# mLSTM running maxima and decays: broadcast by DMA and masked on GpSimd instead of selected and masked by TensorE products

## The chip, the core and the metric

One core of a Trainium2 chip runs the whole program. The metric is the device time of one execution in microseconds (us), the median of several runs.

The engines are named as in the profile: PE is TensorE (matmuls; PEld its weight loads), DVE is VectorE, ACT is ScalarE, POOL is GpSimd, SP is the engine whose queue issues most DMAs. TensorE writes to PSUM, ScalarE and VectorE read it.

## The reference, cut to what matters

The program is one inference step of a two-layer backbone for 128 prompt tokens and 256 latent tokens (three tiles of 128), width 1024. A layer normalises and modulates the tokens, mixes them with three groups of heads that share one input projection (neighbourhood attention, grouped-query attention, a bidirectional mLSTM of 4 heads of size 64), projects back, and applies a SwiGLU. The part around the change is the mLSTM, for each direction and head:

```
b    = cumsum(log_f)
logw = where(causal, b[t] - b[s] + i[s], -inf)
m_t  = max(max_s logw, b + m)                  # running maximum
s    = (q k^T) * exp(logw - m_t)
num  = s v + exp(b + m - m_t) * (C q)          # the decay of the carried state
den  = sum(s) + exp(b + m - m_t) * (n q)
h    = num / max(|den|, exp(-m_t))
```

With a[s] = i[s] - b[s] and M[t] the running maximum of a (started from m), the exponent is a[s] - M[t] where the mask allows it, and the decay is exp(m - M[t]).

## The kernel before, in words

All 384 tokens are on hand at once, and weights stream from HBM. Each projection weight is loaded as fp32 (`raw`, SP's queue), split into a high and a low part (`hi` by ScalarE, line 121; `lo` by VectorE, line 122), and multiplied in three products (`mm3`, lines 111 to 113).

The work of a mixer layer is a hand-written order of steps in `SCHEDULE`, one string a layer; within it TensorE, VectorE and ScalarE execute in the order in which the steps issue. GpSimd's and SP's queues are ordered by a planner. Steps that matter here: `f`, a part of the projections; `t`, a part of the modulation vectors (its sum is in a PSUM tile of tag `sm`); `s`, a part of the norms of heads; `rexp`, `cols`, `krow`, `rsplit`, `cin`, `decay`, `kw`, `cout`, `ogate`, parts of the mLSTM that run once a layer; `E0` to `E3`, `C0` to `C3`, `U0` to `U3`, the exponents, scores and sums of the four mLSTM units. A unit is a pair of heads (j) in one direction (dr).

The rows `m.R1` (the running maxima M, 64 x 384), `m.R2` (a) and `m.R3` hold a head's tokens along the free dimension, at partition 32 dr + head. `cols` transposes R2 and R3 so that a[s] can be a per-partition bias. To have M[t] along the free dimension of all 128 partitions, the kernel multiplies on TensorE:

- `rsplit` splits R1 into a high and a low part, `m.Rh`.
- `m_expo` (step E) multiplies a column of the negated identity `nidr`, broadcast to 128 columns, by Rh: -M[t] in all partitions, into the PSUM tile `E` (tag `pt`). Two more products per head add the mask `trir` through the identity. ScalarE then writes W = exp(E + a[s]), six instructions (line 864).
- `decays` does the same for m - M[t] into `dps` (tag `pt`) for the 64 partitions of each head; ScalarE's exponent gives `decq`, which VectorE multiplies by q.

`m_score` (step C) multiplies keys by queries into the PSUM tile `S` (tag `sc`), and VectorE multiplies W by S (line 877). `m_sum` (step U) sums over keys on TensorE into `nd` (tag `sm`), together with decq times the carried state `CT` that `cin` made out of `Craw`. The PSUM tags `sc`, `pt` and `sm` have one buffer each, `w` (the projections' sums) three. SBUF tiles of tag `m4` (Rm, Rw, Craw, decq, kw, W, ...) share three buffers.

`Ada.gate` already broadcasts a row by way of DRAM: GpSimd stores it to `row` (line 209) and loads it to all 128 partitions as `G` (line 210).

Of the kernel before, what the change touches and what calls it, by code (L numbers as in the profile page):

```python
# [16 lines left out]
D = 1024  # L17
# [29 lines left out]
C_ID, C_SC, C_MNEG, C_COS, C_SIN, C_NID, C_SI, C_SF, C_FL, C_END = (  # L47
    0, 128, 132, 196, 324, 452, 516, 580, 644, 772)
# [3 lines left out]
def hybrid_step(  # L52
# [54 lines left out]
    identr = cp.tile([128, 128], F32R, name="identr")  # L107
    nidr = cp.tile([64, 64], F32R, name="nidr")
    trir = cp.tile([128, 2, 128], F32R, name="trir")
# [154 lines left out]
    def ada_start(pp):  # L264
        """First layer's shift and scale, two feature tiles at a time."""
# [56 lines left out]
    def half_sum(n, h, ss):  # L322
        """Towards 1 / root mean square of two halves of a row, in ss[:, 0]."""
# [48 lines left out]
    def mixers(l, ma, mp, mn, pp, banks, h1T, steps, pairs, tails):  # L372
# [40 lines left out]
        def ahead(n):  # L413
            """Keeps n pairs of weights split before their use, and the loads after them under way."""
# [53 lines left out]
        def tok_first(c0):  # L468
            ps = [pp.tile([128, 512], F32, tag="w", name="tps") for _ in range(3)]
            if l == 0:  # L470
# [27 lines left out]
                xt = [norm_x(0), norm_x(1), norm_x(2, ma.tile([128, D], F32, tag="m4", name="xn2", bufs=3))]  # L498
# [23 lines left out]
                tri = tp.tile([128, 256], F32, tag="g2", name="tri", bufs=4)  # L522
                SP.dma_start(tri, consts[:, C_END:C_END + 256])
                late.enter_context(tc.issue_after(an))
                late.enter_context(tc.issue_after(v))
                V.tensor_copy(identr, ident)
                V.tensor_copy(nidr, cst[0:64, C_NID:C_NID + 64])
                V.tensor_copy(trir, tri.rearrange("p (a b) -> p a b", a=2))
# [18 lines left out]
        # ---- M: mLSTM projections  # L547
# [39 lines left out]
        grows = ma.tile([128, 384], F32, tag="m4", name="grows", bufs=3)  # L587
# [11 lines left out]
        # ---- G: rotary tables with the gains  # L599
# [127 lines left out]
        def out_first():  # L727
            ps, w = {}, {}
            for half, ch, i in [(0, 0, i) for i in range(3)] + [
# [6 lines left out]
                if ch:  # L736
                    if not half:
                        oP.append(ma.tile([128, D], F32, tag="m4", name="oP", bufs=3))
# [18 lines left out]
        # ---- M: gates  # L757
        def gates():
# [3 lines left out]
            m.R1 = mp.tile([64, 384], F32, name="R1")  # L762
# [51 lines left out]
        # ---- M: columns, final states of the prompt  # L814
# [26 lines left out]
        def m_blocks(dr):  # L841
            if dr == 0:
                return [(0, 0, 128, 0), (1, 128, 384, 128), (2, 256, 384, 384)]
            return [(0, 0, 128, 0), (1, 128, 256, 128), (2, 128, 384, 256)]

        def m_expo(u):
            j, dr = pairs_of[u]
            E = pp.tile([128, 2, 512], F32, tag="pt", name="E")
            bl = [(0, 384, 0), (256, 384, 384)] if dr == 0 else [(0, 256, 0), (128, 384, 256)]
            for hd in range(2):  # L850
                r = 32 * dr + 2 * j + hd
                sel = nidr[:, r:r + 1].broadcast_to([64, 128])
                for n, (ta, tb, o) in enumerate(bl):
                    for a in range(2):
                        PE.matmul(E[:, hd, o:o + tb - ta], lhsT=sel, rhs=m.Rh[:, a, ta:tb],
                                  start=n == 0 and a == 0, stop=False)
                PE.matmul(E[:, hd, 0:256].rearrange("p (b t) -> p b t", b=2), lhsT=identr,
                          rhs=trir[:, dr].unsqueeze(1).broadcast_to([128, 2, 128]), start=False, stop=False)
                PE.matmul(E[:, hd, 384:512], lhsT=identr, rhs=trir[:, dr], start=False, stop=True)
            M["W", u] = W = ma.tile([128, 2, 512], F32, tag="m4", name="W", bufs=3)  # L860
            for hd in range(2):
                r = 32 * dr + 2 * j + hd
                for st, ta, tb, o in m_blocks(dr):
                    A.activation(W[:, hd, o:o + tb - ta], E[:, hd, o:o + tb - ta], AF.Exp, bias=m.cols[:, st, r:r + 1])

        def m_score(u):
            j, dr = pairs_of[u]
            S = pp.tile([128, 2, 512], F32, tag="sc", name="S")
            for st, ta, tb, o in m_blocks(dr):
                for ch in range(2):  # L870
                    for hd in range(2):
                        pr = slice(64 * hd, 64 * hd + 64)
                        cc = 64 * ((ch + hd) % 2)
                        PE.matmul(S[cc:cc + 64, hd, o:o + tb - ta], lhsT=kTm[pr, j, st * 128 + cc:st * 128 + cc + 64],
                                  rhs=qTm[pr, j, ta:tb], start=True, stop=True)
# [3 lines left out]
        def m_sum(u):  # L879
# [4 lines left out]
            plan = ([(0, [(0, 0)]), (1, [(1, 128)]), (2, [(1, 256), (2, 384)])] if dr == 0  # L884
                    else [(0, [(0, 0)]), (1, [(1, 128), (2, 256)]), (2, [(2, 384)])])
# [18 lines left out]
            else:  # L904
                ht = ma.tile([128, 3, 2, 64], F32, tag="m4", name="ht", bufs=3)
# [16 lines left out]
        def decays():  # L922
            nid = cst[0:64, C_NID:C_NID + 64]
            dps = pp.tile([128, 2, 512], F32, tag="pt", name="dps")
            for dr in range(2):
                for j in range(2):
                    for hd in range(2):
                        r = 32 * dr + 2 * j + hd
# [562 lines left out]
```

## Time and profile before

| | |
|---|---|
| median of 3 runs | 1025.33 us (1025.22 to 1027.11) |
| span of the profiled execution | 1023.0 us |
| time around that span, to the median of the runs | 2.3 us |
| TensorE busy | 995.2 us, 97% |
| VectorE busy | 620.6 us, 61% |
| ScalarE busy | 469.4 us, 46% |
| GpSimd busy | 60.4 us, 6% |
| moved by DMA | 162.26 MB, mean 159 GB/s |

The span runs from the first to the last instruction of one profiled execution. Busy is the time in which an engine executed something; matmuls are pipelined and overlap, so that TensorE's work is better read from the starts of successive instructions. An idle engine that is not the bottleneck costs nothing; a wait is attributed to the work that ended last before it.

### The profile page before, as it was taken

To read this page: it belongs to the slowest core of one execution; us is meant where nothing else is said; L and a number is where in the kernel's file an instruction comes from. 1 tells how busy PE (TensorE), PEld (TensorE's weight loads), DVE (VectorE), ACT (ScalarE), POOL (GpSimd) and SP (SyncE) were. 2 spreads that over 40 slices of the span, in tenths; PEclk is the share of its full clock that TensorE was granted. 3 is DMA by queue.
4 is the path that set the end of the run, shared out by engine and by line. 5 is a ranking of instruction groups with operands and counts; after the bars stand their busy time and mean duration, and the time that the engine had idled before them with its cause. 6 is when DMAs were issued, how large, how long until landed. Compare 5 with 4: busy or idle time off the path is not lost.

```text
span 1023.0 us, 16943 instructions
## 1 busy us (share of the span) xinstructions
PE 995.2 (97%) x6777; PEld 861.1 (84%) x6777; DVE 620.6 (61%) x1035; ACT 469.4 (46%) x936; POOL 60.4 (6%) x110
## 2 busy tenths in 40 slices
PE   5999999999999999999999999999999999999997
PEld 4778887667999998989987789866799999999996
DVE  3566546667883898976255755666878533333324
ACT  4444424668733333333266444577873323333322
POOL 0310112000000300000010221000000000000000
PEclk9999999999999999999999999999999999999999
DMA  9955568425773777765033662441477344333001
GB/s 324 302 161 168 145 174 270 134 62 189 261 251 124 253 253 225 251 217 162 1 98 101 199 207 48 108 109 42 136 258 244 125 145 144 124 124 124 22 1 62
DMA packets 126831, 162.26 MB, mean 159 GB/s; under 512 B 15184, under 2 KB 89536, under 8 KB 126752
## 3 DMA queue, kind: packets, MB, share of 16 engines
q1 hardware_dynamic: 122256, 154.22, 48.1%
q0 software_dynamic: 4128, 6.80, 2.2%
q8 instruction: 53, 0.87, 0.3%
q10 hardware_dynamic: 368, 0.16, 0.1%
q14 instruction: 26, 0.21, 0.1%
HBM read 158.50 MB, written 2.66 MB: 158 GB/s over the span
## 4 chain that ended last, share of the span: by engine, by line
PE 87%; ACT 4%; DVE 4%; DMA 3%; issue 2%; DVEq 0%; SPq 0%; ACTq 0%
PE gups L111 11%; PE gups L113 11%; PE gups L112 11%; PE facc L111 6%; PE facc L113 6%; PE facc L112 6%; PE tps L111 3%; PE fps L111 2%; PE tps L113 2%; PE tps L112 2%; PE fps L113 2%; PE fps L112 2%; DMA sraw<-in_w_ada_dram 2%; PE sc L997 2%; PE ops L111 2%; PE ptp L1028 2%
## 5 line engine op out<-in xcount | busy, mean ns | idle before, releaser
L122 DVE TENSOR_TENSOR lo<-raw,hi 128x1024 fp32r<-128x1024 f32 x98 | 119.3, 1223 | 66.7 <-ACT hi L121 66.4
L121 ACT ACTIVATE hi<-raw 128x1024 fp32r<-128x1024 f32 x98 | 103.2, 1058 | 90.9 <-PE facc L113 87.1
L111 PE MATMUL gups<-hT,ring 128*128 128x384 f32 x416 | 141.1, 339 | 0.0
L113 PE MATMUL gups<-hT,ring 128*128 128x384 f32 x416 | 140.6, 338 | 0.0
L112 PE MATMUL gups<-hT,ring 128*128 128x384 f32 x416 | 140.4, 338 | 0.0
L182 DVE SCALAR_TENSOR_TENSOR spare<-araw,scol,spare 128x512 f32<-128x512 f32 x168 | 115.8, 748 | 3.7 <-DMA araw<-in_w_ada_dram 3.7
L111 PE MATMUL facc<-hi,f 128*128 128x512 f32 x240 | 95.9, 399 | 0.0
L113 PE MATMUL facc<-hi,f 128*128 128x512 f32 x240 | 94.7, 394 | 0.0
L112 PE MATMUL facc<-lo,f 128*128 128x512 f32 x240 | 94.6, 394 | 0.0
L111 PEld LDWEIGHTS gups<-hT,ring 128*128 128x128 f32 x416 | 78.1, 188 | 0.9 <-issue 0.2
L112 PEld LDWEIGHTS gups<-hT,ring 128*128 128x128 f32 x416 | 78.2, 188 | 0.3
L113 PEld LDWEIGHTS gups<-hT,ring 128*128 128x128 f32 x416 | 78.1, 188 | 0.0
L111 PE MATMUL gups<-hT,xring 128*128 128x384 f32 x224 | 76.0, 339 | 0.0
L113 PE MATMUL gups<-hT,xring 128*128 128x384 f32 x224 | 75.7, 338 | 0.0
L112 PE MATMUL gups<-hT,xring 128*128 128x384 f32 x224 | 75.6, 338 | 0.0
L111 PE MATMUL tps<-hi,hT 128*128 128x512 f32 (+1 forms) x192 | 68.5, 357 | 2.2 <-DVE hT L489 2.2
L113 PE MATMUL tps<-hi,hT 128*128 128x512 f32 (+1 forms) x192 | 65.1, 339 | 0.0
L112 PE MATMUL tps<-lo,hT 128*128 128x512 f32 (+1 forms) x192 | 65.1, 339 | 0.0
L1217 ACT ACTIVATE ring<-spare 128x1024 fp32r<-128x1024 f32 x26 | 27.6, 1060 | 60.8 <-PE gups L112 38.2
L1217 ACT ACTIVATE ring<-rgu 128x1024 fp32r<-128x1024 f32 x26 | 27.6, 1060 | 59.5 <-PE gups L112 34.6
L111 PEld LDWEIGHTS facc<-hi,f 128*128 128x128 f32 x240 | 45.1, 188 | 11.2 <-issue 1.8
L1232 DVE TENSOR_TENSOR sg<-sg,gups 128x384 f32<-128x384 f32 x40 | 22.2, 554 | 52.9 <-PE gups L113 52.9
(318 smaller groups left out, 2057.1 us busy)
## 6 DMA issues: line engine op xcount, KB each, us to landing
araw<-in_w_ada_dram SPq DMA_DIRECT2D x80, 512.0 KB, 4.5
raw<-in_w_down_dram SPq DMA_DIRECT2D x44, 512.0 KB, 4.6
raw<-in_w_in_dram SPq DMA_DIRECT2D x40, 512.0 KB, 5.0
rgu<-in_w_gu_dram SPq DMA_DIRECT2D x20, 1024.0 KB, 5.5
spare<-in_w_gu_dram SPq DMA_DIRECT2D x20, 1024.0 KB, 6.9
sraw<-in_w_ada_dram SPq DMA_DIRECT2D x16, 512.0 KB, 9.3
raw<-in_w_out_dram SPq DMA_DIRECT2D x8, 512.0 KB, 5.3
G<-row POOLq DMA_DIRECT2D x8, 512.0 KB, 5.7
```

Source lines behind the costliest of these rows:

```text
L111: PE.matmul(out, lhsT=wh, rhs=xh, start=start, stop=False)
L112: PE.matmul(out, lhsT=wh, rhs=xl, start=False, stop=False)
L113: PE.matmul(out, lhsT=wl, rhs=xh, start=False, stop=stop)
L121: a = A.activation(hi[:, :n], raw, AF.Copy)
L122: v = V.tensor_tensor(lo[:, :n], raw, hi[:, :n].bitcast(F32), ALU.subtract)
L182: V.scalar_tensor_tensor(acc[:, s], raw[:, k2], scol[:, k, s:s + 1], acc[:, s], ALU.mult, ALU.add)
L997: PE.matmul(sc[cc:cc + 64, hd, u * nk:(u + 1) * nk], lhsT=qT[pr, cc:cc + 64], rhs=kT[pr], start=True, stop=bias is None)
L1028: PE.transpose(pt[:, hd, b * 128:(b + 1) * 128], self.P[:, hd, b * 128:(b + 1) * 128], ident)
L1217: A.activation(hi, rv, AF.Copy)
L1232: V.tensor_tensor(sg, sg, pu, ALU.mult)
```

## The change

R1 becomes the first part of a 640-column tile `R1m`; `rexp` writes M - m into the other 256 columns. GpSimd stores the rows of the eight heads and directions to a DRAM tile `rows` (2 x 4 x 640), and loads from it:

- into `decq`, 64 partitions a head, the decays' rows;
- in a new step `L0` to `L3`, a unit's maxima into W itself, to all 128 partitions, in four blocks of 128 columns per head; GpSimd's `affine_select` then fills the masked places of three of the blocks with +1e30.

Step E is ScalarE alone: W = exp(a[s] - W), in place, again six instructions. `decay` is an exponent in place and the multiply. The products into `E` and `dps`, the step `rsplit`, the constants `identr`, `nidr`, `trir` and the load of the mask go. Tag `m4` has four buffers, the descriptor scratch of GpSimd's DMAs is set to 8192. The order of the blocks in W and S is changed, with the same products in the score and in the sums.

```diff
-        "f f f t f f f t gates scans f f f f t f s f s rexp s f f f f s f f Q0 s f t s f f f s f s f f f t f Q1 f s "
-        "t cols s f krow f f s rsplit cin decay s f kw s f Q2 E0 cout s C0 t s f t s f t E1 s t s ogate C1 s U0 E2 "
+        "f f f t f f f t gates scans f f f f t f s f s rexp L0 s f f f f s f f Q0 s f t s f f f s f s f f f t f Q1 f s "
+        "t cols s f krow f f s cin L1 decay s f kw s f Q2 E0 cout L2 s C0 t s f t s f t E1 s t s ogate C1 s U0 L3 E2 "
...
-        "s f f Q2 f t f t f krow f s cols rsplit kw decay cin f f E0 C0 s cout E1 s ogate C1 f f t U0 f s f t s s "
+        "s f f Q2 f t f t f krow f s cols kw decay cin L1 f f E0 C0 s cout L2 E1 s ogate C1 f f t U0 L3 f s f t s s "
         "E2 U1 C2 f t s t s s s s E3 C3 f t s U2 s f s f f U3 s f s t s s s s hsum s f kT t f s f f t hrstd f hnorm "
...
         def row_exps():
             A.activation(m.R3, m.R3, AF.Exp, scale=-1.0)
-            m.Rm = ma.tile([64, 256], F32, tag="m4", name="Rm", bufs=3)
-            V.tensor_scalar(m.Rm, m.R1[:, 128:384], m0, None, ALU.subtract)
-            m.Rw = ma.tile([64, 128], F32, tag="m4", name="Rw", bufs=3)
+            V.tensor_scalar(m.R1m[:, 384:640], m.R1[:, 128:384], m0, None, ALU.subtract)
+            m.rows = dp.tile([2, 4, 640], F32, name="mrow")
+            for dr in range(2):
+                G.dma_start(m.rows[dr], m.R1m[32 * dr:32 * dr + 4])
+            m.Rw = ma.tile([64, 128], F32, tag="m4", name="Rw", bufs=4)
             A.activation(m.Rw, m.R2[:, 0:128], AF.Exp, bias=m.mend[:, 1:2])
 
-            m.Craw = ma.tile([65, 8, 64], F32, tag="m4", name="Craw", bufs=3)
+            m.decq = ma.tile([128, 2, 2, 256], F32, tag="m4", name="decq", bufs=4)
+            for hd in range(2):
+                G.dma_start(m.decq[64 * hd:64 * hd + 64],
+                            m.rows[:, hd:4:2, 384:640].unsqueeze(0).broadcast_to([64, 2, 2, 256]))
+            m.Craw = ma.tile([65, 8, 64], F32, tag="m4", name="Craw", bufs=4)
...
-        def split_rows():
-            m.Rh = mp.tile([64, 2, 384], F32R, tag="R", name="Rh")
-            A.activation(m.Rh[:, 0], m.R1, AF.Copy)
-            V.tensor_tensor(m.Rh[:, 1], m.R1, m.Rh[:, 0].bitcast(F32), ALU.subtract)
...
+        def m_load(u):
+            j, dr = pairs_of[u]
+            M["W", u] = W = ma.tile([128, 2, 512], F32, tag="m4", name="W", bufs=4)
+            t = 128 if dr else 256
+            for o, a, e in ((0, 0, 384), (384, t, t + 128)):
+                G.dma_start(W[:, :, o:o + e - a],
+                            m.rows[dr, 2 * j:2 * j + 2, a:e].unsqueeze(0).broadcast_to([128, 2, e - a]))
+            diag = W[:, :, 0:384].rearrange("p h (b t) -> p h b t", b=3)
+            G.affine_select(out=diag, in_=diag, pattern=[[0, 2], [0, 3], [-1 if dr else 1, 128]],
+                            compare_op=ALU.is_ge, fill=-NEG, base=0, channel_multiplier=1 if dr else -1)
+
+        def m_keys(dr):
             if dr == 0:
-                return [(0, 0, 128, 0), (1, 128, 384, 128), (2, 256, 384, 384)]
-            return [(0, 0, 128, 0), (1, 128, 256, 128), (2, 128, 384, 256)]
+                return [(0, slice(0, 1), 0, 128), (1, slice(1, 4, 2), 128, 384), (2, slice(2, 3), 256, 384)]
+            return [(0, slice(0, 1), 0, 128), (1, slice(1, 2), 128, 256), (2, slice(3, 1, -1), 128, 384)]
 
         def m_expo(u):
             j, dr = pairs_of[u]
-            E = pp.tile([128, 2, 512], F32, tag="pt", name="E")
-            bl = [(0, 384, 0), (256, 384, 384)] if dr == 0 else [(0, 256, 0), (128, 384, 256)]
+            W = M["W", u].rearrange("p h (b t) -> p h b t", b=4)
             for hd in range(2):
                 r = 32 * dr + 2 * j + hd
-                sel = nidr[:, r:r + 1].broadcast_to([64, 128])
-                for n, (ta, tb, o) in enumerate(bl):
-                    for a in range(2):
-                        PE.matmul(E[:, hd, o:o + tb - ta], lhsT=sel, rhs=m.Rh[:, a, ta:tb],
-                                  start=n == 0 and a == 0, stop=False)
-                PE.matmul(E[:, hd, 0:256].rearrange("p (b t) -> p b t", b=2), lhsT=identr,
-                          rhs=trir[:, dr].unsqueeze(1).broadcast_to([128, 2, 128]), start=False, stop=False)
-                PE.matmul(E[:, hd, 384:512], lhsT=identr, rhs=trir[:, dr], start=False, stop=True)
-            M["W", u] = W = ma.tile([128, 2, 512], F32, tag="m4", name="W", bufs=3)
...
+                for st, bs, ta, tb in m_keys(dr):
+                    if bs.step == -1:
+                        bs = slice(2, 4)
+                    A.activation(W[:, hd, bs], W[:, hd, bs], AF.Exp, scale=-1.0, bias=m.cols[:, st, r:r + 1])
...
         def decays():
-            nid = cst[0:64, C_NID:C_NID + 64]
-            dps = pp.tile([128, 2, 512], F32, tag="pt", name="dps")
-            for dr in range(2):
-                for j in range(2):
-                    for hd in range(2):
-                        r = 32 * dr + 2 * j + hd
-                        PE.matmul(dps[64 * hd:64 * hd + 64, dr, j * 256:(j + 1) * 256],
-                                  lhsT=nid[:, r:r + 1].broadcast_to([64, 64]), rhs=m.Rm, start=True, stop=True)
-            m.decq = ma.tile([128, 2, 2, 256], F32, tag="m4", name="decq", bufs=3)
-            A.activation(m.decq, dps.rearrange("p d (j t) -> p d j t", j=2), AF.Exp)
+            A.activation(m.decq, m.decq, AF.Exp, scale=-1.0)
             V.tensor_tensor(m.decq, m.decq, qTm[:, :, 128:384].unsqueeze(1).broadcast_to([128, 2, 2, 256]), ALU.mult)
...
-    nc = _bacc.Bacc("TRN2", target_bir_lowering=False, num_devices=1)
+    nc = _bacc.Bacc("TRN2", target_bir_lowering=False, num_devices=1,
+                    dynamic_dma_scratch_size=8192)
```

## Rows read from the trace of the kernel before

**Rows 1.** The page: TensorE's busy time; granted clock in 40 slices.

```profile
PE 995.2 (97%) x6777; PEld 861.1 (84%) x6777; DVE 620.6 (61%) x1035; ACT 469.4 (46%) x936; POOL 60.4 (6%) x110
...
PEclk9999999999999999999999999999999999999999
```

**Rows 2.** The page: the chain that ended last, by engine.

```profile
PE 87%; ACT 4%; DVE 4%; DMA 3%; issue 2%; DVEq 0%; SPq 0%; ACTq 0%
```

**Rows 3.** Waits of TensorE, whole span: us in total, times, longest.

```profile
PE adat L236 <- ACT Cout L948: 0.5, 1, 0.5
```

**Rows 4.** Windows: each engine's busy us (x instructions), clock, DMA share, GB/s.

```profile
95.00:125.00 30.00, 29.50 (x323) 24.88 (x322) 17.24 (x43) 15.40 (x41) 3.53 (x5) 1.00 0.47 125
...
598.00:650.00 52.00, 52.00 (x476) 47.22 (x476) 27.30 (x56) 23.92 (x59) 8.03 (x12) 1.00 0.43 110
```

**Rows 5.** The tile E: ns min/median/max of an instruction, first and last start.

```profile
L855 PE MATMUL E<-Rh,nidr x64: 215/276/439, 102.2 to 632.0; 64*128 64x256 f32 x32, 64*128 64x384 f32 x16, 64*128 64x128 f32 x16
```

**Rows 6.** Timeline, TensorE, layer 0: start us, length us, instruction [idle <-releaser].

```profile
96.80 1.94 PE L929 MATMUL dps<-Rm,cst 64*64 64x256 f32 x16
98.67 0.39 PE L111 MATMUL tps<-hi,hT 128*128 128x256 f32 x1
...
102.17 0.79 PE L855 MATMUL E<-Rh,nidr 64*128 64x384 f32 x4
...
104.25 1.11 PE L945 MATMUL cop<-kw,share 128*65 128x64 f32 x16
...
117.33 0.78 PE L855 MATMUL E<-Rh,nidr 64*128 64x384 f32 x4
...
119.62 1.10 PE L874 MATMUL S<-qTm,kTm 64*64 64x128 f32 x24
```

**Rows 7.** Timeline, ScalarE, layer 0.

```profile
109.16 1.06 ACT L121 ACTIVATE hi<-raw 128x1024 fp32r<-128x1024 f32 x1
113.46 1.87 ACT L864 ACTIVATE W<-E,share 128x128 f32<-128x128 f32 x6 [3.24 <-PE E L859]
...
116.60 0.84 ACT L955 ACTIVATE share<-share 128x768 f32<-128x768 f32 x1
```

**Rows 8.** Timeline, VectorE, layer 0.

```profile
118.36 1.21 DVE L877 TENSOR_TENSOR W<-W,S 128x1024 f32<-128x1024 f32 x1
```

**Rows 9.** Timeline, TensorE, layer 1.

```profile
604.56 0.46 PE L914 MATMUL ctp<-cst,Craw 65*128 65x65 f32 x4
...
607.88 0.78 PE L855 MATMUL E<-Rh,nidr 64*128 64x384 f32 x4
...
610.04 1.10 PE L874 MATMUL S<-qTm,kTm 64*64 64x128 f32 x24
...
612.16 0.74 PE L855 MATMUL E<-Rh,nidr 64*128 64x256 f32 x4
...
630.48 0.72 PE L855 MATMUL E<-Rh,nidr 64*128 64x256 f32 x4
```

**Rows 10.** Timeline, ScalarE, layer 1.

```profile
608.15 0.27 ACT L619 ACTIVATE z<-tps 128x128 f32<-128x128 f32 x1
610.15 1.87 ACT L864 ACTIVATE W<-E,share 128x128 f32<-128x128 f32 x6 [1.72 <-PE E L859]
...
612.27 0.59 ACT L948 ACTIVATE Cout<-cop 65x512 f32<-65x512 f32 x1
```

**Rows 11.** Timeline, VectorE, layer 1.

```profile
612.05 1.22 DVE L877 TENSOR_TENSOR W<-W,S 128x1024 f32<-128x1024 f32 x1 [3.06 <-ACT W L864]
...
629.64 1.22 DVE L877 TENSOR_TENSOR W<-W,S 128x1024 f32<-128x1024 f32 x1
```

**Rows 12.** The page: DMA issues, KB each, median us to landing.

```profile
G<-row POOLq DMA_DIRECT2D x8, 512.0 KB, 5.7
```

**Rows 13.** GpSimd by form: busy us, mean ns, idle before <-releasers.

```profile
L210 POOL DMA_DIRECT2D G<-row x8 | 6.2, 770 | 23.7 <-issue 15.6 <-DMA row<-acc 8.1
...
L917 POOL MEMSET CT<- 128x520 f32 x2 | 1.1, 552 | 0.0
```

More of the change, by code (lines that the diff above doesn't have):

```diff
@@ L497, in tok_first @@
                 raws = load_q(0)
-                xt = [norm_x(0), norm_x(1), norm_x(2, ma.tile([128, D], F32, tag="m4", name="xn2", bufs=3))]
+                xt = [norm_x(0), norm_x(1), norm_x(2, ma.tile([128, D], F32, tag="m4", name="xn2", bufs=4))]
                 ws[0] = load_k(wl_in, 0, 2, c0, 512)[:2]
@@ L586, in mixers @@
                               start=k2 == 0 and n == 0, stop=k2 == 1 and n == 1)
-        grows = ma.tile([128, 384], F32, tag="m4", name="grows", bufs=3)
+        grows = ma.tile([128, 384], F32, tag="m4", name="grows", bufs=4)
         A.activation(grows, gps[:, :384], AF.Identity, bias=bg)
@@ L737, in out_first @@
                     if not half:
-                        oP.append(ma.tile([128, D], F32, tag="m4", name="oP", bufs=3))
+                        oP.append(ma.tile([128, D], F32, tag="m4", name="oP", bufs=4))
                     A.activation(oP[i][:, HALVES[half]], ps[half, i], AF.Copy)
@@ L761, in gates @@
             PE.matmul(m.sips[64:128, 1, :384], lhsT=cst[:, C_SF:C_SF + 64], rhs=grows, start=True, stop=True)
-            m.R1 = mp.tile([64, 384], F32, name="R1")
+            m.R1m = mp.tile([64, 640], F32, name="R1")
+            m.R1 = m.R1m[:, 0:384]
             m.R = mp.tile([64, 2, 384], F32, tag="R", name="R")
@@ L868, in m_score @@
             S = pp.tile([128, 2, 512], F32, tag="sc", name="S")
-            for st, ta, tb, o in m_blocks(dr):
+            Sb = S.rearrange("p h (b t) -> p h b t", b=4)
+            for st, bs, ta, tb in m_keys(dr):
                 for ch in range(2):
@@ L873, in m_score @@
                         cc = 64 * ((ch + hd) % 2)
-                        PE.matmul(S[cc:cc + 64, hd, o:o + tb - ta], lhsT=kTm[pr, j, st * 128 + cc:st * 128 + cc + 64],
-                                  rhs=qTm[pr, j, ta:tb], start=True, stop=True)
+                        PE.matmul(Sb[cc:cc + 64, hd, bs], lhsT=kTm[pr, j, st * 128 + cc:st * 128 + cc + 64],
+                                  rhs=qTm[pr, j, ta:tb].rearrange("p (b t) -> p b t", t=128), start=True, stop=True)
             W = M["W", u]
@@ L883, in m_sum @@
             ndv = nd[:, 0:390].rearrange("p (i h e) -> p i h e", i=3, h=2)
-            plan = ([(0, [(0, 0)]), (1, [(1, 128)]), (2, [(1, 256), (2, 384)])] if dr == 0
-                    else [(0, [(0, 0)]), (1, [(1, 128), (2, 256)]), (2, [(2, 384)])])
+            plan = ([(0, [(0, 0)]), (1, [(1, 128)]), (2, [(1, 384), (2, 256)])] if dr == 0
+                    else [(0, [(0, 0)]), (1, [(1, 128), (2, 384)]), (2, [(2, 256)])])
             for ti, terms in plan:
@@ L904, in m_sum @@
             else:
-                ht = ma.tile([128, 3, 2, 64], F32, tag="m4", name="ht", bufs=3)
+                ht = ma.tile([128, 3, 2, 64], F32, tag="m4", name="ht", bufs=4)
                 V.tensor_tensor(ht, ndv[:, :, :, 0:64], rb, ALU.mult)
@@ L922, in decays @@
         def decays():
-            nid = cst[0:64, C_NID:C_NID + 64]
-            dps = pp.tile([128, 2, 512], F32, tag="pt", name="dps")
-            for dr in range(2):
-                for j in range(2):
-                    for hd in range(2):
-                        r = 32 * dr + 2 * j + hd
-                        PE.matmul(dps[64 * hd:64 * hd + 64, dr, j * 256:(j + 1) * 256],
-                                  lhsT=nid[:, r:r + 1].broadcast_to([64, 64]), rhs=m.Rm, start=True, stop=True)
-            m.decq = ma.tile([128, 2, 2, 256], F32, tag="m4", name="decq", bufs=3)
-            A.activation(m.decq, dps.rearrange("p d (j t) -> p d j t", j=2), AF.Exp)
+            A.activation(m.decq, m.decq, AF.Exp, scale=-1.0)
             V.tensor_tensor(m.decq, m.decq, qTm[:, :, 128:384].unsqueeze(1).broadcast_to([128, 2, 2, 256]), ALU.mult)
         def key_weights():
-            m.kw = ma.tile([128, 2, 4, 64], F32, tag="m4", name="kw", bufs=3)
+            m.kw = ma.tile([128, 2, 4, 64], F32, tag="m4", name="kw", bufs=4)
             for dr in range(2):
@@ L961, in head_sums @@
         def head_sums():
-            sq = ma.tile([128, 12, 64], F32, tag="m4", name="sq", bufs=3)
+            sq = ma.tile([128, 12, 64], F32, tag="m4", name="sq", bufs=4)
             hm12 = m.hm12 = m.hml.rearrange("p i h d -> p (i h) d")
@@ L1070, in mask_bias @@
                 hi = m.bias_hi[:, 0:768].rearrange("p (h b c) -> p h b c", h=2, b=6)
-                lo = ma.tile([128, 2, 6, 64], F32R, tag="m4", name="bias_lo1", bufs=3)
+                lo = ma.tile([128, 2, 6, 64], F32R, tag="m4", name="bias_lo1", bufs=4)
             else:
-                m.bias_hi = ma.tile([128, 1024], F32R, tag="m4", name="bias_hi1", bufs=3)
+                m.bias_hi = ma.tile([128, 1024], F32R, tag="m4", name="bias_hi1", bufs=4)
                 m.flipr = m.bias_hi[:, 768:896]
@@ L1132, in mixers @@
         steps = {
-            "gates": gates, "scans": scans, "rexp": row_exps, "krow": key_rows, "cols": columns, "rsplit": split_rows,
+            "gates": gates, "scans": scans, "rexp": row_exps, "krow": key_rows, "cols": columns,
             "cin": states_in, "decay": decays, "kw": key_weights, "cout": states_out, "ogate": out_gate,
@@ L1440, in _shape_constants @@
     P = np.arange(128)
-    o = np.zeros((128, C_END + 256), np.float32)
+    o = np.zeros((128, C_END), np.float32)
     o[:, C_ID:C_ID + 128] = np.eye(128)
-    o[:, C_END:C_END + 128] = np.where(P[:, None] > P[None, :], NEG, 0.0)
-    o[:, C_END + 128:C_END + 256] = np.where(P[:, None] < P[None, :], NEG, 0.0)
     qc = 63 - P % 64
```

20 lines of the change are left out of this document (4 added, 16 removed), and 2 rows, old and new, of the table SCHEDULE.

## The prediction, made before the change was run

> **What bounds the kernel now.** Read the page first. TensorE is busy 97% of the span and its granted clock stands at full speed in all 40 slices [rows 1]; the chain that ended last runs through TensorE for 87% of the span [rows 2]. So the other engines matter only where TensorE waits for them. Next the windows of the two stretches in which the mLSTM units run: in layer 0 TensorE is busy 29.5 of 30 us, in layer 1 52.0 of 52.0, while VectorE and ScalarE are about half busy, GpSimd a sixth or less, and the DMA engines under half [rows 4]. TensorE's waits are mostly at the start of the program; in these stretches the longest is one of 0.5 us, for a PSUM tile that ScalarE still reads [rows 3]. What is to be seen: time here is TensorE's time, almost to the tenth, and the queue of steps is written out by hand, so a TensorE step that is cut pulls in all behind it, until it uncovers a wait on another engine that it used to hide.
>
> The times below are of one profiled execution, whose span is 1023.0 us. The median of the runs is 1025.33, 2.3 us or 0.2% above it; I take those 2.3 us as lying around the span, unchanged, and subtract savings from 1025.3.
>
> **What the change removes.** First, the exponents. An E step is 12 products on TensorE, eight with the rows Rh (64 records over the program [rows 5]) and four with the mask. Matmuls overlap, so durations can't be added; the price is start to start. E0 of layer 0 begins at 102.17 and the next step's first product at 104.25: 2.08 us; E0 of layer 1 from 607.88 to 610.04: 2.16 [rows 6, 9]. Eight units at 2.08 make 16.6 us. Second, the decays: 16 records per layer, from 96.80 to the next step's start at 98.67: 1.87 us [rows 6], twice, 3.7 us. Together **20.4 us of TensorE**. The split of R1 and three small casts at the start go from ScalarE and VectorE, and one 128 KB load from SP's queue; TensorE's projections cover them and no wait of its names them, so they count nothing (at most the split's 0.5 us a layer, were ScalarE late there).
>
> **What it adds off TensorE.** Per layer: two stores of R1's rows, two loads of decq (256 KB each), and for each of four units two broadcast loads (384 and 128 KB) and one select on GpSimd over 128 x 768. All 12 transfers are issued by GpSimd. The kernel's G loads are the same thing, 512 KB from a DRAM row to all partitions: 0.77 us of GpSimd an issue [rows 13], 5.7 us to landing [rows 12]. The 5 MB come on top of engines under half used [rows 4]; the weight loads, asked for two ahead, I leave unchanged; if that cover is gone, a load's delay shows one to one behind the splits. The select has no row. GpSimd's memset of 520 elements a partition takes 0.55 us [rows 13], 0.81 for 768; that is a pass that only writes, and the lower end. A select also reads and compares: three such passes, 2.4 us, I take as upper end of the plain case, and 1.6 as value. (Estimates from that row.) A load thus takes 0.77 + 5.7 + 1.6, about 8 us, from a free buffer to a usable W.
>
> [...]
>
> ScalarE's six exponents of a unit keep their 1.87 us, but read SBUF in place; they no longer wait for TensorE (3.24 us before E1 [rows 7]). The score products and the sums keep their counts and columns, only the order of blocks differs: nothing, as the columns streamed set their time.
>
> **What the cut uncovers.** The tile S (tag sc) has one buffer, so a C step's products can't start before VectorE has multiplied the unit before. I move each chain by what TensorE loses ahead of it.
>
> Layer 0, C2. ScalarE is ready for E1 at 110.22, the end of its weight split; 3.95 us earlier (decays and E0) that is 106.3. From the start of E1's exponents (113.46) through the output gate's two passes (to 117.44) to the end of VectorE's multiply (119.57) is 6.1 us [rows 7, 8]: done at 112.4. TensorE, which started E2 at 117.33 [rows 6], now arrives 6.0 us earlier, at 111.3. Wait: 1.1 us. (Before, E2's products hid it just: S starts at 119.62.)
>
> Layer 1, C1. Only the small cop product lies between C0 and C1. ScalarE is free at 608.42 [rows 10], now at 606.55; exponents 1.87, multiply 1.22 [rows 11]: 609.6. TensorE reached E1 at 612.16 [rows 9], less 1.87 and 2.16: 608.1. Wait: 1.5 us.
>
> Layer 1, C3. The multiply of unit 2 ends at 630.86 [rows 11], TensorE was through at 630.48 with what precedes E3 [rows 9]: 0.4 us.
>
> The wait for Cout's PSUM tile (0.5 us [rows 3]): TensorE comes 2.08 earlier and ScalarE's exponents stay before the copy; between 0 and 2.1 more, I take 0.5, since the exponents start earlier as well.
>
> Late loads. L0 and layer 0's L1 are issued long ahead of use. Layer 1's W1 takes the buffer of Craw, free when the ctp transposes end (605.02, now 603.15 [rows 9]); usable at 611.2. ScalarE, done with Cout at 612.86, moves with E0's exponents by 3.6 (they began at 610.15 and now at 606.55) to 609.3 [rows 10]. So ScalarE stands 2 us, and the output gate and the copies that free the projections' PSUM tiles queue behind it; TensorE has two projection parts and U0 before it needs them. I take 1.0 us, between 0 and 4.7 (if the issue also stands behind a G load's wait for its row, 8.1 us in three times [rows 13]). W2 and W3 of both layers get their buffers at cout and at U0; by the same walk they come between 1.3 us early and 2 late; behind the exponents wait weight splits, used a part or two later. I take 1.5 us for the four, between 0 and 8.
>
> Sum: 20.4 - (1.1 + 1.5 + 0.4 + 0.5 + 1.0 + 1.5 = 6.0) = 14.4 us. **1025.3 - 14.4 = 1010.9; I say 1011.**
>
> **Rivals.**
>
> *All of it hidden* (chance 0.20). If loads land in time and the chains shift more freely than I walked, the cut counts whole: 1025.3 - 20.4 = 1005. For it: half-idle ScalarE and VectorE [rows 4]. Against it: the one buffer of S; E2 hid a multiply that ended 0.05 us before S.
>
> *Loads late everywhere* (0.14). GpSimd runs its queue in order; a select that waits for its landing holds the next unit's issues, the G loads and the outputs behind it. At 2.4 us a select and one such wait (2.7) more, five loads (W1 of layer 1, W2 and W3 of both) come 3.5 us later, of which TensorE feels half to all: 9 to 17 us lost, 1018 to 1025. Against: GpSimd's order before shows issues placed by readiness, and it is busy for under a sixth of these stretches.
>
> [...] As a mechanism here, which I put inside this rival with 0.04 of its chance: VectorE stands for each select, 6.4 us a layer, with 24.7 of 52 us idle to take it [rows 4]; if half reaches TensorE, 6 us in all: 1017. No row of before shows GpSimd computing beside VectorE long enough to judge.
>
> *Slower: the select is the bound* (0.08). One mechanism: a select several times its plain price. The cut less the waits without late loads is 16.9 us, five late loads share it: 3.4 us of TensorE each. With about 2 us of slack before TensorE feels a load, that is 5.4 us beyond plan: a select of 7 us or more breaks even, one of 10 us gives 1025 + 5 x 3 = 1040. For it: nothing in the trace bounds a select from above. Against: memset's pace, nine times quicker.
>
> *No change* (0.04): the late loads add up to about that break-even; within 0.2%, 2 us, about what a measurement here can tell from nothing.
>
> My own case has 0.54, and covers 1007 to 1017. Its faster companions bring faster by over 0.2% to 0.54 + 0.20 + 0.14 = 0.88; same 0.04; slower 0.08. The range: 1004.5 takes in the full cut, 1020 half of the late-load rival; outside remain about 2 in 10.
>
> **What will show it.** Right: no E or dps products; TensorE's busy time about 20 us less; its waits now name S after VectorE's W multiply, about 1 us each, in C2 of layer 0 and C1 of layer 1; ScalarE's exponents waiting for GpSimd for 0 to 3 us, most in layer 1's E1; a select of 1 to 2.4 us; G loads and weight loads landing as before. Wrong: selects of 5 us or more; ScalarE waiting over 4 us for W2 and W3, with TensorE waiting for splits or copies behind it; TensorE idle over 8 us in the two stretches; or a lower granted clock there.

## The result and the profile after

The changed kernel takes 1008.97 us, the median of 4 runs (1008.34 to 1009.37); the kernel before took 1025.3 us beside it. The ratio is 0.9836, 95% interval 0.9822 to 0.985: 16.3 us faster. The prediction was 1011.0 us with a range of 1004.5 to 1020. In the profiled executions, on which the terms below go, the span fell from 1023.0 to 1007.6, by 15.4 us. Every timed execution lies 1.7 to 1.8 us above its own span, in both kernels; the profiled one of the kernel before was about 0.5 us faster than the median and that of the changed kernel 0.4 us slower, so the spans fall by 0.9 us less than the medians.

The page of the changed kernel, for [rows 1, 2, 12] (busy times, the chain by engine, a row of the DMA issues):

```profile
PE 974.6 (97%) x6649; PEld 844.5 (84%) x6649; DVE 620.2 (62%) x1030; ACT 469.9 (47%) x934; POOL 85.7 (9%) x142
...
PE 80%; ACT 5%; DVE 3%; issue 2%; DVEq 0%; ACTq 0%
...
G<-row POOLq DMA_DIRECT2D x8, 512.0 KB, 4.8
```

TensorE has 20.6 us less of busy time and is still busy 97% of a shorter span. GpSimd has 25.3 us more, VectorE and ScalarE the same as before.

The windows of the changed kernel over the same stretches as [rows 4] (busy time of PE, PEld, DVE, ACT, POOL, then granted clock, DMA share, GB/s):

```profile
95.00:125.00 30.00, 27.29 (x333) 24.09 (x332) 19.01 (x44) 16.83 (x47) 13.04 (x15) 1.00 0.81 224
...
598.00:650.00 52.00, 47.01 (x426) 43.73 (x427) 32.34 (x59) 28.06 (x70) 10.08 (x14) 1.00 0.49 123
```

TensorE was full in these two stretches and now stands for 2.7 and 5.0 us in them; the granted clock still reads 1.00 in both. The DMA engines went from 0.47 to 0.81 in the first.

TensorE's waits in the changed kernel, whole span (us in total, times, longest), those that belong to the change:

```profile
PE S L872 <- DVE W L875: 3.3, 3, 1.7
...
PE cop L934 <- DVE kw L927: 1.2, 1, 1.2
...
PE nd L890 <- DVE hml L901: 0.9, 1, 0.9
...
PE ctp L912 <- DVE share L828: 0.7, 1, 0.7
```

The wait for Cout [rows 3] is gone; in the same layer a wait of 0.41 us is new, for VectorE's sum `acc` at the modulation vectors. The waits listed have their places in TensorE's timeline of the changed kernel (start, length, instruction, idle before and releaser), with three milestones: the gates' products `gps` of each layer, and the first keys of the attention behind the mLSTM of layer 1, `kps`:

```profile
47.63 2.79 PE L577 MATMUL gps<-hT,wg_raw 128*32 128x384 f32 x32 [0.28 <-DMA wg_raw<-in_w_in_dram]
...
99.94 1.13 PE L934 MATMUL cop<-kw,share 128*65 128x64 f32 x16 [1.16 <-DVE kw L927]
...
111.71 1.10 PE L872 MATMUL S<-qTm,kTm 64*64 64x128 f32 x24 [0.69 <-DVE W L875]
...
544.38 2.79 PE L577 MATMUL gps<-hT,wg_raw 128*32 128x384 f32 x32
...
593.59 0.46 PE L912 MATMUL ctp<-cst,Craw 65*128 65x65 f32 x4 [0.72 <-DVE share L828]
...
600.77 1.10 PE L872 MATMUL S<-qTm,kTm 64*64 64x128 f32 x24 [1.68 <-DVE W L875]
...
610.95 0.63 PE L890 MATMUL nd<-share,W 128*128 128x65 f32 x4 [0.90 <-DVE hml L901]
...
616.97 1.10 PE L872 MATMUL S<-qTm,kTm 64*64 64x128 f32 x24 [0.96 <-DVE W L875]
...
650.00 0.44 PE L1112 MATMUL kps<-cst,kTn 128*128 128x128 f32 x2
```

The same milestones in the timeline of the kernel before:

```profile
49.06 2.79 PE L585 MATMUL gps<-hT,wg_raw 128*32 128x384 f32 x32 [1.17 <-DMA wg_raw<-in_w_in_dram]
...
554.25 2.79 PE L585 MATMUL gps<-hT,wg_raw 128*32 128x384 f32 x32
...
665.53 0.44 PE L1123 MATMUL kps<-cst,kTn 128*128 128x128 f32 x2
```

Subtract: 1.43 us are gained before any mLSTM step runs, 8.44 between the two gate products (layer 0), 5.66 more up to the keys of layer 1. That is 15.53, the difference of the spans to 0.1 us, so next to nothing is gained or lost behind it. Each layer lost 10.19 us of TensorE work (half of the predicted 20.4). Layer 0 gives back 0.69 + 1.16 = 1.85 in the waits above, layer 1 0.72 + 1.68 + 0.90 + 0.96 = 4.26. 20.38 - 6.11 + 1.43 = 15.7, against 15.5 measured: two tenths are unassigned. (Cout's wait that went, 0.45 us, and the new one for `acc`, 0.41, cancel.)

The tile W in the changed kernel, on the engines that make it (ns min/median/max, first and last start):

```profile
L861 ACT ACTIVATE W<-W,share x48: 386/388/507, 99.3 to 620.7; 128x128 f32<-128x128 f32 x32, 128x256 f32<-128x256 f32 x16
L841 POOL DMA_DIRECT2D W<-mrow x16: 722/726/760, 79.4 to 611.6; - x16
L844 POOL TENSOR_SCALAR_AFFINE_SELECT W<-W x8: 862/894/1892, 88.3 to 615.0; 128x768 f32<-128x768 f32 x8
...
DMA to landing us min/median/max: 4.0/5.8/9.4
```

A select takes 0.86 us, and up to 1.89 in some places (below). ScalarE waits for a select twice, 2.67 us for tile 1 of layer 1 and 0.25 us for tile 3 of layer 0; the other six are ready when it comes.

The changed kernel was profiled a second time (e5 below; span 1007.4). There tile 1 of layer 1 landed sooner, ScalarE waited 1.22 us for it, and TensorE did not wait for `hml` at all; the waits for kw (1.16), ctp (0.72) and the first two for S (0.69, 1.68) are the same, the third is 0.34. But behind the wait of 1.68, which ends at 600.77, the granted clock was lower: it reads 0.54 from 602 to 604, where TensorE ran 11 products, and 1.00 with 18 products in the first profile. The window of the second (columns as above):

```profile
602.00:604.00 2.00, 2.00 (x11) 2.00 (x11) 0.00 (x0) 1.97 (x7) 1.95 (x3) 0.54 1.16 294
```

So the 0.90 for `hml` and the 0.96 for the third S are of one execution; another execution of the same kernel lost clock in their place, and layer 1's stretch came out nearly as long (105.36 us between the milestones, 105.62 in the first profile).

### The profile page after: what moved, and what is told of

The parts are those of the page before. It is cut to its first block, busy times and chain, and to the rows that moved or that the text cites. A ratio compares the mean times of both kernels' runs of the same rounds, so it can differ in the third digit from the quotient of the medians.

```text
span 1007.6 us, 16738 instructions
## 1 busy us (share of the span) xinstructions
PE 974.6 (97%) x6649; PEld 844.5 (84%) x6649; DVE 620.2 (62%) x1030; ACT 469.9 (47%) x934; POOL 85.7 (9%) x142
## 4 chain that ended last, share of the span: by engine, by line
PE 80%; ACT 5%; DVE 3%; issue 2%; DVEq 0%; ACTq 0%
PE gups L108 11%; PE gups L110 11%; PE gups L109 11%; PE facc L108 6%; PE facc L110 6%; PE facc L109 6%; PE fps L108 2%; PE sc L986 2%; PE ops L108 2%; PE fps L110 2%; PE fps L109 2%; PE ptp L1017 2%; PE tps L108 2%; PE ops L110 2%; PE ops L109 2%
## 5 line engine op out<-in xcount | busy, mean ns | idle before, releaser
L1221 DVE TENSOR_TENSOR sg<-sg,gups 128x384 f32<-128x384 f32 x40 | 22.1, 552 | 53.1 <-PE gups L110 53.1
```

The costliest lines, as they stand in the source:

```text
L1221: V.tensor_tensor(sg, sg, pu, ALU.mult)
```

## Experiments

Ratios are to the kernel before, run on the same chip. A second set of runs of the changed kernel (beside e6 to e8) gave 1008.43 us, ratio 0.9833 [0.9818, 0.9847]; it is what those three are held against. An interval is some 3 us wide, so the differences of about 1 us that e1, e6, e9 and e10 have to the changed kernel are not shown by the times; there the traces have to decide. What was expected of e5:

> The changed kernel itself, on the same chip as the next three, to compare them with: 1009, within 0.8.

**The four buffers and the scratch setting alone (e4).** The kernel before with `bufs=4` in tag `m4` and `dynamic_dma_scratch_size=8192`, and nothing else of the change.

> The kernel before with only the fourth buffer of tag m4 and the smaller descriptor scratch. If the gain is TensorE's products, this part alone gives nothing: 1025.3, within 1. Rival, that the extra buffer relaxes waits and is part of the gain: 1023 or less.

Measured: 1025.3 us, 1.0001 [0.9992, 1.001]. They are worth nothing by themselves.

**The decays back on TensorE (e2).**

```diff
-            A.activation(m.decq, m.decq, AF.Exp, scale=-1.0)
+            dps = pp.tile([128, 2, 512], F32, tag="pt", name="dps")
...
+                        PE.matmul(dps[64 * hd:64 * hd + 64, dr, j * 256:(j + 1) * 256], lhsT=nid[:, r:r + 1]
+                                  .broadcast_to([64, 64]), rhs=m.R1m[:, 384:640], start=True, stop=True)
+            A.activation(m.decq, dps.rearrange("p d (j t) -> p d j t", j=2), AF.Exp)
```

> The changed kernel with the decays made by TensorE again, the exponents by DMA and mask. If the gain is TensorE's time, start to start, the two decay steps cost 2 x 1.87 = 3.7 us, less what they cover of the two new waits beside them (cop for kw 1.16, ctp for a copy 0.72): 1011 to 1012.7. Rival, that the decays' products cost nothing because TensorE had slack there: 1009.

Measured: 1012.16 us (1011.11 to 1013.15), 0.9873 [0.9859, 0.9886]. By the medians the decays by DMA are worth 3.2 us (3.8 by the ratios) where their products cost TensorE 3.7, and what is left in e2 (the exponents with their masks, and the start) 12.8 against the kernel before beside it. With the decays' products back, TensorE's wait for ctp is gone and the one for kw is 0.7.

**The loads late (e3).** In `SCHEDULE`, each step L directly ahead of its E.

```diff
-t cols s f krow f f s cin L1 decay s f kw s f Q2 E0 cout L2 s C0 t s f t s f t E1 s t s ogate C1 s U0 L3 E2
+t cols s f krow f f s cin decay s f kw s f Q2 L0 E0 cout s C0 t s f t s f t L1 E1 s t s ogate C1 s U0 L2 E2
```

> The changed kernel with each unit's load step placed directly ahead of its exponent step in the written order. The load takes about 8 us from issue to a usable W, so by the theory that the load is hidden only because it is issued early, ScalarE stands 5 to 9 us at three or four of the eight units and TensorE feels half or more: 1017 to 1027. Rival, that nothing waits for the loads (ScalarE and VectorE are half idle): 1009 to 1010.

Measured: 1030.72 us (1029.97 to 1031.46), 1.0054 [1.004, 1.0068]: slower than the kernel before, and above both expectations. TensorE's waits in this kernel:

```profile
PE S L872 <- DVE W L875: 7.0, 2, 6.6
PE adat L233 <- ACT Cout L937: 6.8, 1, 6.8
PE adap L214 <- ACT share L676: 4.6, 1, 4.6
```

Its windows in layer 0 (columns as above):

```profile
100.00:105.00 5.00, 1.66 (x35) 1.23 (x33) 0.00 (x0) 0.40 (x1) 1.94 (x3) 0.87 1.01 278
105.00:110.00 5.00, 1.57 (x8) 1.57 (x9) 1.79 (x4) 2.65 (x8) 2.83 (x4) 0.50 0.17 58
110.00:115.00 5.00, 5.00 (x47) 4.23 (x50) 1.71 (x3) 3.49 (x11) 2.30 (x4) 0.60 0.74 175
115.00:120.00 5.00, 4.59 (x84) 3.67 (x76) 3.73 (x10) 4.14 (x12) 0.73 (x1) 1.00 0.76 241
```

ScalarE waited 20.8 us for selects, 12.1 at the longest, and what is queued behind it (Cout, the shares) held TensorE: the waits above, with 0.7 each for cop and ctp, are 19.8 us against 6.1, 13.7 more. TensorE's busy time is 982.7, 8.1 more than in the changed kernel with the same products: behind the wait of 6.8 the granted clock reads 0.50 from 105 to 110, 0.60 to 115 and 1.00 from there, and a product of `tps` took 0.41 us for 0.28; behind the one of 6.6, in layer 1, it reads 0.50 from 620 to 625. 13.7 + 8.1 = 21.8 of the span's 22.1. So it is the early place of L0 to L3 in the order that hides the loads; the late ones were paid twice here, 13.7 us in stalls and 8.1 in busy time.

**The select left out (e6).** The kernel leaves out the mask, so its results are not the program's.

```diff
-            G.affine_select(out=diag, in_=diag, pattern=[[0, 2], [0, 3], [-1 if dr else 1, 128]],
-                            compare_op=ALU.is_ge, fill=-NEG, base=0, channel_multiplier=1 if dr else -1)
```

> The changed kernel without GpSimd's select: the mask is left out of the exponents, so future positions count in the maxima's weights. By the theory that the select only delays W by 0.9 us and slows VectorE's weight split beside it (1.89 us instead of 1.22 at one place), the wait of cop for kw falls from 1.2 to about 0.5 us, that of unit 1's sums in layer 1 from 0.9 to 0, and the time by 1 to 2 us: 1007 to 1008. Rival, that the select is what keeps the loads late everywhere: 5 us or more less, 1004 or below.

Measured: 1007.73 us (1007.42 to 1008.01), 0.9825 [0.981, 0.9839], 0.7 us under e5; the span is 1.8 lower. TensorE's wait for `hml` (0.9) is gone, as it is in e5's trace with the selects in place; that for kw is 0.73, those for S still sum to 2.6. The wait for kw leads to VectorE. GpSimd's timeline of the changed kernel there:

```profile
96.49 1.89 POOL L844 TENSOR_SCALAR_AFFINE_SELECT W<-W 128x768 f32<-128x768 f32 x1 [4.04 <-DMA W<-mrow]
```

VectorE's timeline of the changed kernel:

```profile
96.43 1.23 DVE L922 TENSOR_TENSOR decq<-decq,qTm 128x1024 f32<-128x1024 f32 x1
97.57 1.89 DVE L119 TENSOR_TENSOR lo<-raw,hi 128x1024 fp32r<-128x1024 f32 x1
99.38 0.74 DVE L927 TENSOR_TENSOR kw<-kml,share 128x256 f32<-128x256 f32 x2
```

VectorE's timeline without the select:

```profile
96.47 1.23 DVE L919 TENSOR_TENSOR decq<-decq,qTm 128x1024 f32<-128x1024 f32 x1
97.61 1.22 DVE L119 TENSOR_TENSOR lo<-raw,hi 128x1024 fp32r<-128x1024 f32 x1
98.75 0.75 DVE L924 TENSOR_TENSOR kw<-kml,share 128x256 f32<-128x256 f32 x2
```

Beside a select, the split took 1.89 instead of 1.22 us, kw started 0.63 later, and TensorE stood 1.16 instead of 0.73. The select itself took 1.89 instead of 0.86. Of the 0.4 us that TensorE stood less here the layer kept little: from gate products to gate products it takes 496.65 us without the select, 496.75 and 496.81 in the two profiles with it.

**The select twice (e9).** The same call a second time, which changes no value.

> Each of the eight selections on GpSimd is made twice, so a selection costs about 0.86 us more where nothing disturbs it. My theory: three of the eight tiles arrive with little room (ScalarE's exponent waited 2.7 us for the selection of tile 1 in layer 1 and 0.25 us for tile 3 in layer 0, and the product with S is late three times), the others have more than 0.9 us of room; so +1 to +3 us, 1009.5 to 1011.5. Rival, that the selections set the pace of the mixers: eight times 0.86 and more where VectorE is held up, +7 us or more, 1015.5. Rival, that the selections are wholly hidden: 1008.5.

Measured: 1010.11 us (1009.51 to 1011.86), 0.9848 [0.9832, 0.9865]: 1.1 us over the changed kernel (0.0012 by the ratios), where eight full prices would be 7. The waits for S are the same 3.3; the one for kw went from 1.2 to 2.2 us, and there VectorE's two passes of that place took 1.82 and 1.88 us. VectorE's and GpSimd's timelines in e9:

```profile
96.89 1.82 DVE L924 TENSOR_TENSOR decq<-decq,qTm 128x1024 f32<-128x1024 f32 x1
...
96.77 0.86 POOL L844 TENSOR_SCALAR_AFFINE_SELECT W<-W 128x768 f32<-128x768 f32 x1 [3.45 <-DMA W<-mrow]
```

TensorE's:

```profile
101.00 1.84 PE L936 MATMUL cop<-kw,share 128*65 128x64 f32 x16 [2.18 <-DVE kw L929]
102.77 1.96 PE L874 MATMUL S<-qTm,kTm 64*64 64x128 f32 x24
```

Behind this wait the two steps took 1.84 and 1.96 us instead of 1.13 and 1.10. So of the 2.6 us that layer 0 lost in this profile (the slowest execution of the four) 1.0 is the wait and 1.6 the longer steps; that the clock made them longer, as in e7, is the author's estimate. In TensorE's waits the second select shows in this one place, where it runs beside VectorE.

**Two PSUM buffers for S (e1).**

```diff
-            S = pp.tile([128, 2, 512], F32, tag="sc", name="S")
+            S = pp.tile([128, 2, 512], F32, tag="sc" if u % 2 else "pt", name="S")
```

> The changed kernel with the score tile S of even units put into the PSUM tag that the exponents used to fill (pt), so that S has two buffers. If the gain was cut by TensorE waiting for S's one buffer (0.69 + 1.68 + 0.96 us in the changed kernel's trace), these waits go and the time falls by about 3 us, to 1006 (1005 to 1007.5). Rival: the wait only moves to the next consumer of W, and the time stays at 1009.

Measured: 1008.28 us (1007.35 to 1010.1), 0.9837 [0.9824, 0.9851]; profiled span 1005.6. All three waits for S are gone, so their cause, the one buffer, is shown. Time hardly shows it, against the expected 1005 to 1007.5: the profiled execution gained 2.0 us and the median 0.7, of 3.3, and by the ratios (0.9837 for 0.9836) nothing is gained. In the trace the wait of layer 0 reappears at the modulation vectors (for VectorE's `acc`, 1.0 us instead of 0.4), in layer 1 part of it at the sums (nd for `hml`, 1.4).

**The mask's load put back (e7).** The load of `tri` and its cast, read by nothing, at their old place in the code.

```diff
+                tri = tp.tile([128, 256], F32, tag="g2", name="tri", bufs=4)
+                SP.dma_start(tri, consts[:, C_END:C_END + 256])
...
+                V.tensor_copy(trir, tri.rearrange("p (a b) -> p a b", a=2))
```

> The changed kernel with the old kernel's 128 KB load of the mask and its cast put back, read by nothing. TensorE's gate products wait 1.2 us for their weights' load in the kernel before and 0.3 in the changed one. If the mask's load stood in front of that load, the wait comes back: about 1 us more, 1010. Rival, that the start of the program only varies from execution to execution: 1009, with a wait of 0.5 or less.

Measured: 1013.04 us (1012.43 to 1013.55), 0.9878 [0.9862, 0.9895], 4.6 over e5 where 1 was expected. SP's queue (start, time, issue) around the gates' weight `wg_raw`, in the kernel before:

```profile
42.50 0.46 SPq L523 DMA_DIRECT2D tri<-in_consts_dram  x1
43.01 0.50 SPq L579 DMA_DIRECT2D wg_raw<-in_w_in_dram  x1
```

In the changed kernel:

```profile
41.52 0.37 SPq L126 DMA_DIRECT2D raw<-in_w_in_dram  x1
41.94 0.78 SPq L571 DMA_DIRECT2D wg_raw<-in_w_in_dram  x1
```

In this one:

```profile
35.29 0.34 SPq L520 DMA_DIRECT2D tri<-in_consts_dram  x1
41.54 3.78 SPq L126 DMA_DIRECT2D raw<-in_w_in_dram  x2
45.36 0.48 SPq L575 DMA_DIRECT2D wg_raw<-in_w_in_dram  x1
```

The planner set the load elsewhere than before, with two weight loads ahead of `wg_raw`, so this isn't the old start again. It shows that `wg_raw` is what TensorE waits for there and that its place in the queue prices the wait: issued at 41.94, 43.01 and 45.36, it made `gps` wait 0.28, 1.17 and 2.74 us. In the two traces of kernels with the mask's load directly ahead of `wg_raw` (the kernel before and e4) the wait is 1.17 and 1.54 us and `gps` starts at 49.06 and 49.30; in the ten without that load the wait is 0 to 0.63 us and the start 47.57 to 48.24. The wait of e7 cost more than itself. TensorE's timeline in e7:

```profile
50.09 4.07 PE L581 MATMUL gps<-hT,wg_raw 128*32 128x384 f32 x32 [2.74 <-DMA wg_raw<-in_w_in_dram]
```

The windows of e7 at that place (columns as above):

```profile
50.00:52.00 2.00, 1.91 (x13) 0.69 (x17) 0.00 (x0) 0.00 (x0) 0.39 (x1) 0.50 1.10 321
52.00:54.00 2.00, 2.00 (x24) 0.68 (x16) 0.00 (x0) 0.00 (x0) 0.00 (x0) 0.82 0.89 316
```

Behind the stall the granted clock reads 0.50 and 0.82 in these two windows, and the same 32 products took 4.07 instead of 2.79 us. By the end of `gps` e7 is 3.7 us behind the changed kernel.

**The waits opened (e8).** Two buffers for S, `ctp` into tag `pt`, and steps moved: kw ahead of the decay (layer 0), the load L1 to the front and kw behind `decay` and `cin` (layer 1).

```diff
-f f s cin L1 decay s f kw s f Q2 E0
+f f s cin L1 kw decay s f s f Q2 E0
...
-f krow f s cols kw decay cin L1 f f E0
+f krow f s cols L1 decay cin kw f f E0
```

> The changed kernel with three edits against its new waits: the score tile of even units and the state transposes (ctp) in the PSUM tag that the exponents left free; in layer 0 kw before decay; in layer 1 the second load step before decay, kw after cin. The waits of S (3.3 us), of cop for kw (1.2) and of ctp (0.7) go; a wait for VectorE's sums in tag sm stays or grows to 1 us in layer 0, as the run with two buffers of S showed. 3.5 to 4.5 us below the changed kernel, 1004.5 to 1005.5. Rival, that the waits only move on: within 1.5 us of the changed kernel.

Measured: 1006.93 us (1006.49 to 1007.92), 0.9818 [0.9804, 0.9833]. The waits for S and ctp are gone, and none for kw is named, but cop still stands 0.73 us, with no releaser shown. 1.5 us came of it by the medians (2.2 by the spans), where 3.5 to 4.5 were expected: the sums now wait for `hml` 2.2 us (0.9 before, none in e5). The rival, that the waits only move on, is nearer.

**The loads on SP's queue (e10).** `SP.dma_start(W...)` in place of `G.dma_start`.

> The eight broadcast loads go out on SyncE's queue, among the weight loads, in place of GpSimd's. My theory: on GpSimd's queue they hold up nothing that the path needs, and on SyncE's queue a load that waits for its buffer or its row holds the weight loads behind it; the weights are about one buffer ahead there, so +0 to +6 us, 1008.5 to 1014.5, with new waits of TensorE for weights. Rival, that GpSimd's queue is what makes a load slow (its median 5.8 us to landing): landings drop under 4.5 us, the waits of the products with S shrink, and the time falls by 1 to 3 us, 1005.5 to 1007.5.

Measured: 1007.56 us (1007.45 to 1008.23), 0.9827 [0.9812, 0.9841]. Neither theory holds whole: no new wait for weights shows, and the landings are not shorter (median 6.1 us). What changed is layer 1's tile 1. On GpSimd's queue its load is issued behind a G load that waits for its row; in the changed kernel:

```profile
595.06 0.78 POOL L207 DMA_DIRECT2D G<-row  x1 [2.80 <-DMA row<-acc]
595.84 1.47 POOL L841 DMA_DIRECT2D W<-mrow  x2
...
601.85 0.86 POOL L844 TENSOR_SCALAR_AFFINE_SELECT W<-W 128x768 f32<-128x768 f32 x1 [3.54 <-DMA W<-mrow]
```

On SP's queue the load goes out at 594.70, its select runs at 598.77, ScalarE's waits for selects fall from 2.9 to 0.2 us, and TensorE's for `hml` is gone. Part of this is the landing: e10's program runs 0.6 us later up to here, so that the load goes out some 1.7 us sooner and its select runs some 3.7 us sooner. In e5 the load, issued as late as before, already landed soon enough for a wait of 1.2 us.

**Both (e11).** e8 with the loads on SP's queue.

> The version with the opened waits (1006.9) and the eight loads on SyncE's queue together. My theory: the loads on SyncE's queue gained 1 us because layer 1's tile 1 no longer stood behind a G load on GpSimd's queue, and the opened waits gained 1.5 us elsewhere; the two add, except that opening the waits had already moved that tile's load ahead: 1005.0 to 1006.5, and VectorE's late sums (nd, 2.2 us with the opened waits alone) shrink to under 1 us. Rival, that what is left is set by VectorE's and ScalarE's own chain in these stretches: 1006.9, unchanged, with the same late sums.

Measured over five runs: 1005.52 us (1005.2 to 1007.43), 0.9814 [0.98, 0.9827]; of TensorE's waits for S, kw, ctp and `hml` only 0.5 us for `hml` is left (2.2 in e8), beside the 0.7 of cop without a releaser. It is the fastest version here, 2 to 3.5 us under the change as made by ratios or medians; the two intervals just overlap.

## Why the prediction came out as it did

Its own case held. What it gave for each step, and the traces:

| step of the sum | predicted, us | measured, us |
|---|---|---|
| TensorE's work cut | 20.4 | busy time 20.6 less |
| C2 of layer 0 waits for S | 1.1 | 0.69 |
| C1 of layer 1 waits for S | 1.5 | 1.68 |
| C3 of layer 1 waits for S | 0.4 | 0.96 (e5: 0.34) |
| Cout's PSUM tile | 0.5 | 0, and the 0.45 of before gone |
| W1 of layer 1 late | 1.0 | 0.90 (e5: 0, with a granted clock of 0.54 behind the wait for S) |
| W2 and W3 late | 1.5 | 0; ScalarE 0.25 once |
| cop waits for kw, layer 0 | not in the sum | 1.16 |
| ctp waits for the columns, layer 1 | not in the sum | 0.72 |
| modulation sums wait for `acc`, layer 0 | not in the sum | 0.41 |
| the start, with the mask's load gone | counted as nothing | 1.43 gained |

- **The cut and the place of the waits** were right: start-to-start prices of [rows 6, 9] gave TensorE's saving to 0.2 us, and moving each chain by what TensorE loses ahead of it found the three waits for S. e1 shows that S's one buffer makes them.
- **The losses sum to 6.1 for 6.0, by luck in part**: 2.0 us of terms that didn't come stand against 1.9 of waits that the walk did not look at. It followed the tiles that the change touches (S, W, Cout), and not the small steps beside them, kw and ctp, which the products of the decays and exponents had covered as well: with the decays' products back, e2 has no wait for ctp.
- **The term that was mis-sized** is "they count nothing" for the mask's 128 KB load. It stood directly ahead of `wg_raw` on SP's queue, and TensorE waited 1.17 us there; the prediction looked for a wait that names the mask and not for what was queued behind its load. The forecast missed by 1.9 us. 1.0 of it lies in the spans (14.4 against 15.4), which the 1.43 gained at the start more than cover: 0.89 of that is the shorter wait for `wg_raw`, the rest is TensorE arriving earlier, and which part of it is the mask's load is not shown. That this load makes the wait longer is borne out by the two traces with it against those without it, and e7 shows that the place of `wg_raw` in the queue sets it; e7 did not bring back the old start itself.
- **The 2.3 us "around the span, unchanged"** were not that. The time around the span is 1.7 to 1.8 us in every execution, and the other 0.5 was the difference between the profiled execution and the median. With a profile of the changed kernel on the other side of its median, this is the other 0.9 us of the miss: chance, and no property of the change.
- **Late loads.** The price of a load was near: landing 5.8 us for the predicted 5.7 (4.0 to 9.4 for the loads of 384 and 128 KB), a select of 0.86 to 1.89 for 1.6. The loads of W2 and W3 were on time all the same but for 0.25 us once, where the walk had put 1.5. W1's delay has the cause named in brackets, a G load waiting for its row, in part (e10 takes TensorE's wait away), and in part a landing time that differs from execution to execution (2.67 and 1.22 us of ScalarE's wait in two profiles of the same kernel).
- **The rivals.** "All of it hidden" is out for the change as made, by the waits for S; only e11, with the waits opened, comes near the 1005 that it gave (1005.5). "Loads late everywhere" did not happen here, but e3 shows that the mechanism is real once the loads stand late: 21.8 us, more than its 7 to 14 over the forecast. "The select is the bound" needed 7 us a select and got 0.9; e9, with twice the selects, costs 1.1. That VectorE stands for each select, priced at 6 us, was the author's estimate, and no run shows it for each; the runs showed a split of 1.89 us for 1.22 beside one select, and where it counts, at kw, 0.4 us in the changed kernel and 1.45 in e9 (2.18 for 0.73), with 1.6 of longer steps behind it.

ScalarE's six exponents, predicted at 1.87 us, take 2.06 from SBUF; it moved no term by more than 0.2. Open: two tenths between the waits and the milestones; whether two buffers for S gain any time; and how often an execution of the changed kernel loses clock behind the wait of 1.68, as e5's did (0.54) and the first profile did not (1.00).

## What to carry to other kernels

With TensorE busy 97% of the span, the steps cut from it were worth their start-to-start time (20.4 us), less the waits of every neighbour whose lead they had hidden (6.1 us): walk the small steps beside the change too, not only its own tiles. Don't count a removed load as nothing on its queue: look at what was issued right behind it and who waits for that (here `wg_raw`, for which TensorE waited 1.17 us before and 0.28 after). A broadcast through DRAM with its mask took 5 to 10 us here from its issue to the end of its select, so its place in the order decided whether the kernel came out 16.3 us faster than with the products that it replaces (1008.97 us) or slower (e3, 1030.72).

## What the runs showed of the hardware that was not expected

- Waits of TensorE of 2.7 us (e7) and of 6.8 and 6.6 us (e3) were each followed by a stretch with a granted clock of 0.50, and products there took longer (`gps` 4.07 for 2.79 us in e7, one of `tps` 0.41 for 0.28 in e3; 8.1 us of busy time over the whole of e3). Behind the wait of 2.2 us in e9 cop and S took 1.84 and 1.96 for 1.13 and 1.10. The same wait of 1.68 us in the same kernel was followed by a clock of 0.54 in one profile (e5) and of 1.00 in the other, so one profile does not tell whether a short wait costs clock.
- Where a select on GpSimd overlapped VectorE's multiply of the decays or its split of a weight, the one that started second took longer. In the changed kernel the decays' multiply starts at 96.43 and takes its usual 1.23 us, the select starts at 96.49 and takes 1.89 instead of 0.86, and the split behind it 1.89 instead of 1.22. In e9 the select starts first, at 96.77, and takes 0.86; the multiply starts at 96.89 and takes 1.82.
- The same broadcast load issued on SP's queue takes 0.46 us an issue for GpSimd's 0.73, and lands no sooner (6.1 against 5.8 us).
